# Attention of a block: four heads at a time, or all eight with their matmuls in pairs

## The chip, the core and the metric

The kernel runs on one core of one Trainium2 chip. The metric is the device time of one execution in microseconds; times are medians of several runs. The engines are called as in the profile: PE (matrix engine; PEld its weight loads), DVE (VectorE), ACT (ScalarE), POOL (GpSimd), SP (whose queue starts the transfers).

## What is computed

A decoder layer: RWKV-7 time mixing and sliding-window attention side by side on 2048 positions and 16 meta tokens, then a gated MLP with a convolution. The change is in the attention: eight query heads, two key/value heads (four query heads share one), head size 64, blocks of 128 positions. A query sees the 16 meta keys, the block before and its own (272 columns), a bias by distance, and a sink that takes part in the softmax alone.

```python
s_meta = jnp.einsum('bnqhgd,bmhd->bhgnqm', qb, meta_k)
s_band = jnp.einsum('bnqhgd,bnkhd->bhgnqk', qb, kband)
...
s = jnp.concatenate([s_meta, s_band], axis=-1).astype(jnp.float32) * scale + bias.astype(jnp.float32)
s = jnp.where(mask_all, s, MASK_VALUE)
...
m = jnp.maximum(jnp.max(s, axis=-1, keepdims=True), sink)
e = jnp.exp(s - m)
prob = (e / (jnp.sum(e, axis=-1, keepdims=True) + jnp.exp(sink - m))).astype(v.dtype)
o = (jnp.einsum('bhgnqm,bmhd->bnqhgd', prob[..., :N_META], meta_v)
     + jnp.einsum('bhgnqk,bnkhd->bnqhgd', prob[..., N_META:], vband))
```

## The kernel before

The kernel has two phases. The first does everything up to the residual `h2`, in nine groups of positions: blocks 0 and 1 (block 0 holds the meta tokens, 16 queries), seven groups of two full blocks, and block 16 alone. The second phase is the MLP (tiles up, dn, o).

A group runs the steps of a list, `ORDER` (`FIRST` and `LAST` for the first and last group). A capital letter is the group's own step, a small one the same step of the group before. B and N begin a group (transposes tp, operands xh and xl), F0 to F3 compute the features of a pair of RWKV heads (matmuls g, pz, pa, pg, pss, spr, pb), P0 to P3 prepare the chunk matrices (sc, vp, kbtp), I0 and I1 invert them in 31 steps on DVE (tm, tt) behind transfers (nd, nt, td), C0 and C1 run the recurrence over chunks (xp, ma, cb, yp), K makes queries and keys (g, qt, kt), A is attention, and j or J the output projection (o).

`attention_block` takes a block and a list of halves. A half is the four query heads of one key/value head; its queries and keys lie in partitions 0 to 63 (j = 0) or 64 to 127 (j = 1), the slice `js`. `A00` is the first half of the group's first block, `A01` its second half, `A1` both halves of the second block, one after the other. For each half:

- four score matmuls ps<-kt,q (64 rows, 272 columns), each in a bank of its own, emptied into `pr` by one DVE instruction that adds the bias and takes the maximum (L794);
- a softmax on DVE and ACT (L796 to L806); `pm` holds the probabilities of the meta keys;
- one transpose of `pm` and eight of `pr` (pt), copied out by ACT (L818, L828) and DVE (L826);
- the output `po`: two matmuls with the values of the block before and of its own (po<-pt,vb, 512 columns, 64 output partitions), four with the meta values (po<-pt,metav, 128 columns each), then ah on ACT (L840) and al on DVE (L841).

`pr` has one buffer, so a half's first eviction needs the earlier half's transposes to be through. The tiles ps, pt and po, and those of the P steps (sc, vp, kbtp), share two PSUM banks, the tag "at", handed out in the order of the program text. The score and value matmuls are fp32; each leaves two PE records.

Every matmul goes through a `Queue`: matmuls of one queue keep their order (`qc` has attention, `qp` the P steps, `qb` the chain, `qa` the large products). How the queues are mixed on PE, and all other engines' order, is set when the program is built, by a list scheduler that takes the ready instruction of highest priority; priority follows the program text, and `high_priority` raises it.

## Time and profile before

| | us |
|---|---|
| median of three runs | 3100.51 (3096.43 to 3104.7) |
| the profiled execution | 3101.82 |
| its span | 3100.0 |
| PE busy | 2834.1 (91%) |
| PEld busy | 2396.3 (77%) |
| DVE busy | 2105.8 (68%) |
| ACT busy | 1188.0 (38%) |
| POOL busy | 1107.3 (36%) |

The first phase ends where the first up product starts, at 1611.2 us of the span. A PE record's length overlaps with its neighbours, since matmuls are pipelined; what one costs a full engine is read from its start to the start of the next. A bracket at a row's end tells how long the engine stood idle before it, and what ended that.

### The profile page before, as it was taken

The numbers are of one execution on the slowest core, as the hardware profiler recorded it, in microseconds if no ns is written. First come the engines' busy times: TensorE is split into PE (matmuls) and PEld (weight loads), VectorE is DVE, ScalarE is ACT, GpSimd is POOL, SyncE is SP. The second block draws the span as 40 slices with busy tenths as digits, with TensorE's granted clock in tenths as the row PEclk, the third lists the DMA queues.
The fourth block names the chain that finished last, engine by engine and source line by source line (L and its number), as shares of the span: only waits on it lengthen the run. The fifth ranks groups of instructions, "written<-read, shape, count | busy, mean of one in ns | idle before, by whom it ended". The sixth has DMA issues, their size and how long they took to land.

```text
span 3100.0 us, 55199 instructions
## 1 busy us (share of the span) xinstructions
PE 2834.1 (91%) x19749; PEld 2396.3 (77%) x19749; DVE 2105.8 (68%) x6008; ACT 1188.0 (38%) x2758; POOL 1107.3 (36%) x1246
## 2 busy tenths in 40 slices
PE   6789898989999999999859999999899999989998
PEld 5567586777777776777548898888899999888887
DVE  5576766667666766666758878787655655766666
ACT  3344433334343433333234443434433333433343
POOL 3322311111111111111146665656444444554554
PEclk8799999989999999999969999999999999999999
DMA  6676677557676767776754343434644444565564
GB/s 216 211 213 187 208 233 233 179 166 231 183 242 183 242 186 226 194 228 192 246 209 156 146 153 133 156 129 162 232 149 139 155 156 140 189 215 177 201 212 159
DMA packets 302198, 586.43 MB, mean 189 GB/s; under 512 B 150570, under 2 KB 154266, under 8 KB 301924
## 3 DMA queue, kind: packets, MB, share of 16 engines
q1 hardware_dynamic: 301924, 582.90, 58.0%
q8 instruction: 157, 2.57, 0.3%
q14 instruction: 117, 0.96, 0.1%
HBM read 483.98 MB, written 98.79 MB: 188 GB/s over the span
## 4 chain that ended last, share of the span: by engine, by line
PE 61%; DVE 15%; DMA 13%; issue 3%; ACT 3%; SPq 3%; POOL 1%; DVEq 0%; ACTq 0%; POOLq 0%
PE up L86 17%; PE dn L86 13%; PE g L86 12%; PE o L86 5%; DMA o<-kept 4%; PE po L86 3%; SPq L587 2%; DMA wraw<-in_wup 2%; PE ma L86 2%; DVE t L997 2%; PE ps L86 2%; DVE tw L1058 2%; DMA w<-kept 2%; DVE t L999 1%; DMA nt<-nd 1%
## 5 line engine op out<-in xcount | busy, mean ns | idle before, releaser
L86 PE MATMUL up<-ah,o 128*128 128x386 f32 (+2 forms) x3696 | 882.7, 324 | 49.9 <-DMA o<-kept 29.0
L86 PEld LDWEIGHTS up<-ah,o 128*128 128x128 f32 x3696 | 652.4, 192 | 61.6 <-issue 11.6
L86 PE MATMUL up<-al,o 128*128 128x386 f32 (+2 forms) x1848 | 596.9, 323 | 6.9 <-DVE al L913 6.9
L86 PE MATMUL g<-xh,w 128*128 128x256 f32 x2016 | 425.8, 301 | 18.7 <-ACT w L170 7.3
L86 PEld LDWEIGHTS g<-xh,w 128*128 128x128 f32 x2016 | 334.7, 198 | 51.6 <-issue 19.8
L86 PEld LDWEIGHTS up<-al,o 128*128 128x128 f32 x1848 | 354.8, 192 | 8.8 <-DVE al L913 7.7
L1031 DVE TENSOR_TENSOR acc<-acc,dn 128x512 f32<-128x512 f32 x360 | 242.4, 684 | 114.9 <-PE dn L86 113.9
L86 PE MATMUL dn<-dh,gh 128*128 128x512 f32 x704 | 279.7, 397 | 29.0 <-DVE acc L1031 26.4
L1069 POOL TENSOR_TENSOR o<-wraw,o 128x512 fp32r<-128x512 f32 x198 | 269.5, 1361 | 99.0 <-ACT o L1068 72.2
L86 PE MATMUL g<-xl,w 128*128 128x256 f32 x1008 | 300.2, 298 | 3.1 <-DVE xl L145 3.1
L86 PE MATMUL dn<-dh,gl 128*128 128x512 f32 x704 | 276.6, 393 | 0.7 <-POOL gl L1006 0.7
L86 PE MATMUL dn<-dl,gh 128*128 128x512 f32 x704 | 276.3, 393 | 0.0
L156 POOL TENSOR_TENSOR dl<-wraw,dh 128x1024 fp32r<-128x1024 f32 x66 | 158.7, 2424 | 203.3 <-ACT dh L155 203.3
L997 DVE SCALAR_TENSOR_TENSOR t<-c,cols,t 128x384 f32<-128x384 f32 (+1 forms) x198 | 169.7, 858 | 79.5 <-ACT t L995 77.4
L86 PEld LDWEIGHTS g<-xl,w 128*128 128x128 f32 x1008 | 199.7, 198 | 14.6 <-issue 6.6
L1006 POOL TENSOR_TENSOR gl<-t,gh 128x384 fp32r<-128x384 f32 (+1 forms) x132 | 134.8, 1021 | 145.4 <-ACT gh L1005 145.4
L592 DVE TENSOR_TENSOR tm<-nt,tt 128x60 f32<-128x60 f32 (+36 forms) x558 | 128.9, 231 | 83.2 <-DMA w<-kept 28.3
L86 PEld LDWEIGHTS dn<-dh,gh 128*128 128x128 f32 x704 | 133.1, 189 | 65.4 <-DVE acc L1031 36.0
L676 POOL TENSOR_TENSOR sw<-S,wc 128x128 f32<-128x128 f32 x66 | 28.5, 432 | 421.1 <-DVE S L677 314.8
L1068 ACT ACTIVATE o<-wraw 128x512 fp32r<-128x512 f32 x198 | 121.8, 625 | 132.4 <-PE up L86 117.5
L995 ACT ACTIVATE t<-c,cols 128x384 f32<-128x384 f32 (+1 forms) x198 | 125.9, 667 | 106.9 <-DVE c L1112 102.1
L86 PE MATMUL g<-w,xh 128*128 128x256 f32 (+3 forms) x544 | 151.7, 362 | 13.9 <-ACT w L170 8.3
(283 smaller groups left out, 5672.3 us busy)
## 6 DMA issues: line engine op xcount, KB each, us to landing
w<-kept SPq DMA_DIRECT2D x448, 512.0 KB
o<-kept SPq DMA_DIRECT2D x176, 512.0 KB
wraw<-in_wup SPq DMA_DIRECT2D x88, 512.0 KB
kept<-o SPq DMA_DIRECT2D x88, 512.0 KB
wraw<-in_wdn SPq DMA_DIRECT2D x66, 512.0 KB
kept<-w SPq DMA_DIRECT2D x56, 512.0 KB
wraw<-in_wup SPq DMA_DIRECT2D x44, 256.0 KB
xt<-in_x SPq DMA_DIRECT2D x16, 512.0 KB
```

Source lines behind the costliest of these rows:

```text
L86: self._pin(self.nc.tensor.matmul(*args, **kw))
L156: nc.gpsimd.tensor_tensor(lo, raw, hi.bitcast(F32), op=ALU.subtract)
L587: nc.sync.dma_start(nt[p0:p0 + H], ndv[:, b * 32:b * 32 + 32, b * 32:b * 32 + 32])
L592: V.tensor_tensor(t, bc(nt[0:np_, s, s + 1:32], j, 1), tt[0:np_, 0:j, s:s + 1].to_broadcast([np_, j, m]), op=ALU.mult)
L995: A.activation(o, c[:, 2:half + 2], AF.Identity, bias=cols[:, C_CB + j:C_CB + j + 1], scale=cols[:, C_CW0 + j:C_CW0 + j + 1])
L997: V.scalar_tensor_tensor(o, c[:, 1:half + 1], cols[:, C_CW1 + j:C_CW1 + j + 1], o, op0=ALU.mult, op1=ALU.add)
L999: V.scalar_tensor_tensor(o, c[:, 0:half], cols[:, C_CW2 + j:C_CW2 + j + 1], o, op0=ALU.mult, op1=ALU.add)
L1006: P.tensor_tensor(gl[:, hs], ts[0], gh[:, hs].bitcast(F32), op=ALU.subtract)
L1031: nc.vector.tensor_tensor(t[:, hs], t[:, hs], ps, op=ALU.add)
L1058: V.tensor_tensor(t, x, y, op=ALU.subtract)
L1068: A.activation(hi, w, AF.Copy)
L1069: P.tensor_tensor(lo, w, hi.bitcast(F32), op=ALU.subtract)
```

## The change

`attention_block` takes all eight heads of a block at once, and the list's steps A00 and A01 become one, A0, where A00 stood. `pr`, `m8`, `l8`, `e8`, `pm` are twice as wide, `metav` has 128 partitions, `pt1` and `pt2` have two buffers. Four times, two banks are taken and two score matmuls are issued, one of each half, in partitions 0 to 63 and 64 to 127; the one whose bank was emptied last comes first, and the second has `follow`, a priority raised by 100000. The two halves' value products go to partitions 0 to 63 and 64 to 127 of one bank, in turn. One transpose serves `pm` of all eight heads, one ah and one al the block. The squares of K take `pr`'s buffer, the squares of N take the projection's junk buffer, and in P the two matmuls of a pair change places.

```diff
-ORDER = "B F0 P0 F1 P1 c1 K I0 F2 A00 P2 F3 P3 A01 A1 I1 j C0 N".split()
+ORDER = "B F0 P0 F1 P1 c1 K I0 F2 A0 P2 F3 P3 A1 I1 j C0 N".split()
 LAST = "B F0 P0 F1 P1 c1 F2 P2 I0 F3 K P3 I1 A0 C0 j C1 J".split()
-FIRST = "B F0 P0 F1 P1 I0 K F2 A00 P2 F3 P3 A01 A1 c1 I1 j C0".split()
+FIRST = "B F0 P0 F1 P1 I0 K F2 A0 P2 F3 P3 A1 c1 I1 j C0".split()
...
-    def matmul(self, *args, **kw):
-        self._pin(self.nc.tensor.matmul(*args, **kw))
+    def matmul(self, *args, follow=False, **kw):
+
+        if follow:
+            with self.tc.high_priority(FOLLOW):
+                self._pin(self.nc.tensor.matmul(*args, **kw))
+        else:
+            self._pin(self.nc.tensor.matmul(*args, **kw))
...
-        junk = pool.tile([128, D // 2], mybir.dt.bfloat16, tag="junk", name="junk", bufs=1)
+        junk = pool.tile([128, D // 2], mybir.dt.bfloat16, tag="jk2", name="junk", bufs=1)
...
-        self.metav = ap([64, 4, 128], F32, "metav")
+        self.metav = ap([128, 4, 128], F32, "metav")
...
-                for hd, ps in enumerate(pss):
+                for hd, ps in reversed(list(enumerate(pss))):
...
-            for h in range(1, 4) if b == 0 else ():
-                nc.sync.dma_start(self.metav[16 * h:16 * h + 16, h, :], self.metav[0:16, 0, :])
-            sq = sp.tile([128, 640], F32, tag="qsq", name="qsq")[0:rows]
+            for x in range(1, 8) if b == 0 else ():
+                nc.sync.dma_start(self.metav[16 * x:16 * x + 16, x % 4, :], self.metav[0:16, 0, :])
+            sq = sp.tile([128, 640], F32, tag="pr", name="qsq", bufs=1)[0:rows]
...
-    def attention_block(self, blk, ctx, halves):
+    def attention_block(self, blk, ctx):
...
+        js = [slice(j * 64, j * 64 + 64) for j in range(2)]
...
+        def bank(name):
+            return self.psum.tile([128, 512], F32, tag="at", name=name, bufs=2)
...
-            pr = sp.tile([128, 4, 272], F32, tag="pr", name="pr", bufs=1)
...
-                ps = self.psum.tile([128, 512], F32, tag="at", name="ps", bufs=2)
-                T.matmul(ps[0:nq, 0:nk], self.q[js, h, q0:q0 + nq], kt[js, 0:nk], start=True, stop=True)
...
+        pr = sp.tile([128, 8, 272], F32, tag="pr", name="pr", bufs=1)
+        m8, l8, e8 = [sp.tile([128, 8], F32, tag=t, name=t, bufs=2)[0:nq] for t in ("m8", "l8", "e8")]
+        sink = self.cols[0:nq, C_SINK:C_SINK + 8]
+        for h in range(4):
+            pss = [bank("ps") for _ in range(2)]
+            turn = ((1, 0), (0, 1))[h % 2]
+            for j in turn:
+                T.matmul(pss[j][0:nq, 0:nk], self.q[js[j], h, q0:q0 + nq], kt[js[j], 0:nk], start=True, stop=True,
+                         follow=j == turn[1])
+            for j in turn:
+                ps, x = pss[j], 4 * j + h
...
-                    V.tensor_tensor_reduce(pr[0:nq, h, 0:nk], ps[0:nq, 0:nk], bt, 1.0, sink[:, h:h + 1],
-                                           ALU.add, ALU.max, m4[:, h:h + 1])
...
+                    V.tensor_tensor_reduce(pr[0:nq, x, 0:nk], ps[0:nq, 0:nk], bt, 1.0, sink[:, x:x + 1],
+                                           ALU.add, ALU.max, m8[:, x:x + 1])
+        V.tensor_tensor(e8, sink, m8, op=ALU.subtract)
+        V.tensor_scalar(m8, m8, -1.0, None, op0=ALU.mult)
+        A.activation(e8, e8, AF.Exp)
...
+        pm = sp.tile([128, 8, 16], F32, tag="pm", name="pm")[0:nq]
+        V.tensor_tensor(pm, pr[0:nq, :, 0:16], bc(l8, 16, 2), op=ALU.mult)
+        for x in range(8) if b else ():
+            V.tensor_scalar(pr[:, x, 16:], pr[:, x, 16:], l8[:, x:x + 1], None, op0=ALU.mult)
...
+            po0, pv = pt0, ps[:, 0:128]
+            T.transpose(pv, pm.rearrange("p h k -> p (h k)"), self.ident)
...
-                for c, (pt, vv) in enumerate(zip(pts, (vprev, vb))):
-                    T.matmul(ps[js], vv[:, js], pt, start=c == 0, stop=False)
-                for h in range(4):
-                    T.matmul(po[:, h, :], self.metav[:, h, js], pt0, start=False, stop=h == 3)
-            hv = ctx["ah"][js, :, q0:q0 + nq]
-            A.activation(hv, po, AF.Copy)
-            V.tensor_tensor(ctx["al"][js, :, q0:q0 + nq], po, hv.bitcast(F32), op=ALU.subtract)
...
+                pts[c].append(pt)
+        ps = bank("po")
+        po = ps.rearrange("p (h t) -> p h t", h=4)[:, :, 0:nq]
...
+            for c, vv in enumerate((vprev, vb)):
+                for j in range(2):
+                    T.matmul(ps[js[j]], vv[:, js[j]], pts[c][j], start=c == 0, stop=False, follow=j == 1)
+            for h in range(4):
+                for j in range(2):
+                    T.matmul(po[js[j], h, :], self.metav[js[j], h, js[j]], pt0[js[j]], start=False, stop=h == 3,
+                             follow=True)
+        hv = ctx["ah"][:, :, q0:q0 + nq]
+        A.activation(hv, po, AF.Copy)
+        V.tensor_tensor(ctx["al"][:, :, q0:q0 + nq], po, hv.bitcast(F32), op=ALU.subtract)
```

What the scheduler makes of it is seen on PE. Behind P3 of a group with two full blocks come, before, the scores of the first block's second half. They stand alone among g's and chain steps (ps are scores; ma and cb the chain; the number is that of the tile):

```order
L86 MATMUL ps_8154<-kt2_117,q_7387 128x272
L86 MATMUL g_8879<-xl_8784,w_8880 128x256
L86 MATMUL g_8879<-xh_8783,w_8880 128x256
L86 MATMUL g_8879<-xh_8783,w_8894 128x256
L86 MATMUL ps_8157<-kt2_117,q_7387 128x272
L86 MATMUL ma_8644<-vu_6755,kbt_6950 64x64 x2
L86 MATMUL ma_8644<-vu_6755,kbt_7156 64x64 x2
L86 MATMUL cb_8645<-vu_6755,ms_6926 64x64 x2
L86 MATMUL cb_8645<-vu_6755,ms_7132 64x64 x2
L86 MATMUL g_8879<-xl_8784,w_8894 128x256
```

There, after, come the scores of the second block:

```order
L92 MATMUL ps_8089<-kt3_118,q_7284 128x272
L92 MATMUL ma_8470<-vu_6652,kbt_6847 64x64 x2
L92 MATMUL ma_8470<-vu_6652,kbt_7053 64x64 x2
L92 MATMUL cb_8471<-vu_6652,ms_6823 64x64 x2
L92 MATMUL cb_8471<-vu_6652,ms_7029 64x64 x2
L90 MATMUL ps_8088<-kt3_118,q_7284 128x272
L92 MATMUL ps_8094<-kt3_118,q_7284 128x272
L92 MATMUL ma_8505<-S0_127,ar_6811 64x64 x2
L92 MATMUL ma_8505<-S0_127,ar_7017 64x64 x2
L92 MATMUL ma_8505<-vu_6652,ms_6823 64x64 x2
L92 MATMUL ma_8505<-vu_6652,ms_7029 64x64 x2
L92 MATMUL cb_8506<-S0_127,ar_6811 64x64 x2
```

Tiles ps_8089 and ps_8088 are a pair (heads of j = 1 and j = 0), 8094 and 8095 the next, 8101 the first of the third. The four steps of ma and of cb have come between the two of a pair, and no g is left between the scores.

At the first block's first scores, behind the key transposes of the same group, before:

```order
L86 MATMUL g_7764<-xl_6586,w_7779 128x256
L86 MATMUL g_7764<-xh_6585,w_7779 128x256
L89 MATMUL kt_7574<-ident_61,qk_7456 128x128
L86 MATMUL ps_7847<-kt2_117,q_7387 128x272
L86 MATMUL ps_7850<-kt2_117,q_7387 128x272
L86 MATMUL g_7960<-xh_6585,w_7961 128x256
```

And after:

```order
L95 MATMUL qt_7465<-ident_61,qk_7353 128x128 x4
L92 MATMUL ps_7745<-kt2_117,q_7284 128x272
L90 MATMUL ps_7744<-kt2_117,q_7284 128x272
L95 MATMUL kt_7471<-ident_61,qk_7353 128x128
L92 MATMUL g_7931<-xh_6482,w_7932 128x256
L92 MATMUL g_7931<-xl_6483,w_7932 128x256
```

The two of before read the same rows, heads 0 and 1 of j = 0; the two of after are a pair of both halves and stand before kt.

The output of a half on PE in a group with two full blocks, before:

```order
L86 MATMUL g_9045<-xh_8783,w_9046 128x256
L86 MATMUL ma_8714<-S0_127,ar_6914 64x64
L86 MATMUL po_8196<-pt2_8194,vb2_121 64x512
L86 MATMUL po_8196<-pt0_8178,metav_123 64x128 x4
L86 MATMUL ps_8209<-kt3_118,q_7387 128x272
L86 MATMUL ma_8714<-S0_127,ar_6914 64x64
```

And the output of the second block of the group that stands above, after:

```order
L92 MATMUL po_8167<-pt1_8144,vb2_121 64x512
L90 MATMUL po_8167<-pt1_8151,vb2_121 64x512
L92 MATMUL po_8167<-pt2_8158,vb3_122 64x512
L92 MATMUL g_8775<-xh_8644,w_8790 128x256 x2
L92 MATMUL g_8775<-xl_8645,w_8790 128x256
L92 MATMUL g_8775<-xh_8644,w_8790 128x256 x2
L92 MATMUL g_8775<-xl_8645,w_8790 128x256
L92 MATMUL g_8775<-xh_8644,w_8790 128x256
L92 MATMUL pz_8819<-wa_8769,dup_106 128x256
L92 MATMUL pa_8823<-wa_8769,dup_106 128x256
L90 MATMUL po_8167<-pt2_8165,vb3_122 64x512
L90 MATMUL po_8167<-pt0_8135,metav_123 64x128 x8
```

Before, the second value product and the four meta products of the half stand together, and the next half's scores behind them. After, three value products stand together, the fourth comes behind g, pz and pa, and then the eight meta products. From the first up product on, PE's order is the same in both programs.

## Rows read from the trace of the kernel before

**Rows 1.** Busy time by stretch: us, PE PEld DVE ACT POOL, PEclk, DMA share, GB/s.
```profile
300.00:1500.00 1200.00, 1130.02 (x9810) 872.23 (x9810) 820.97 (x3406) 462.86 (x1349) 192.03 (x288) 0.96 0.69 210
1500.00:1611.00 111.00, 71.41 (x490) 48.63 (x488) 68.80 (x236) 32.50 (x89) 26.05 (x23) 0.71 0.64 221
1611.00:3100.00 1489.00, 1400.38 (x7736) 1292.63 (x7736) 1030.57 (x1622) 573.69 (x993) 802.05 (x815) 0.98 0.48 166
```

**Rows 2.** PE groups, whole span: xcount | busy us, mean ns | idle before, releasers.
```profile
L86 PE MATMUL ps<-kt,q 64*128 64x272 f32 (+1 forms) x272 | 93.3, 435 | 6.1 <-DVE m L794 5.6 <-ACT vu L562 0.2 <-DVE tm L592 0.2
...
L86 PE MATMUL po<-pt,vb 128*64 128x512 f32 x128 | 67.2, 627 | 1.6 <-DVE last L419 1.5
```

**Rows 3.** PE in time order, 711 to 717: start us, us, what, xcount [idle before <-releaser].
```profile
712.90 0.72 PE L86 MATMUL ps<-kt,q 64*128 64x272 f32 x2
713.55 0.39 PE L86 MATMUL g<-xl,w 128*128 128x256 f32 x1
713.78 0.40 PE L86 MATMUL g<-xh,w 128*128 128x256 f32 x2
714.01 0.28 PE L86 MATMUL g<-xl,w 128*128 128x256 f32 x1
...
716.31 0.45 PE L86 MATMUL ma<-vu,kbt 128*64 128x64 f32 x8
716.59 0.40 PE L86 MATMUL cb<-vu,ms 128*64 128x64 f32 x8
```

**Rows 4.** PE in time order, 730 to 737.
```profile
731.13 1.07 PE L86 MATMUL po<-pt,vb 128*64 128x512 f32 x2
732.13 0.70 PE L86 MATMUL pg<-gd,gup 128*128 128x256 f32 x2
...
736.03 1.08 PE L86 MATMUL po<-pt,metav 64*64 64x128 f32 x8
737.04 0.72 PE L86 MATMUL ps<-kt,q 64*128 64x272 f32 x2
```

**Rows 5.** PE in time order, 754 to 756.
```profile
754.38 1.90 PE L86 MATMUL po<-pt,vb 128*64 128x512 f32 x4 [1.53 <-DVE last L419]
756.21 1.08 PE L86 MATMUL po<-pt,metav 64*64 64x128 f32 x8
```

**Rows 6.** PE in time order, 678 to 680.
```profile
678.79 0.70 PE L86 MATMUL pz<-wa,dup 64*128 64x256 f32 x2
679.42 0.93 PE L86 MATMUL xp<-T,ms 32*32 32x32 f32 x30
```

**Rows 7.** PE in time order, 725 to 726.
```profile
725.06 0.48 PE L86 MATMUL pz<-wa,dup 64*128 64x256 f32 x1
725.07 0.48 PE L86 MATMUL pa<-wa,dup 64*128 64x256 f32 x1
...
725.69 0.39 PE L86 MATMUL g<-xh,w 128*128 128x256 f32 x1
```

**Rows 8.** PE in time order, 1511 to 1512.
```profile
1511.12 0.45 PE L86 MATMUL ma<-S,ar 64*64 64x64 f32 x8
1511.40 0.40 PE L86 MATMUL ma<-vu,ms 64*64 64x64 f32 x8
```

**Rows 9.** Waits of PE from 300 to 1500: us in total, times, longest us.
```profile
PE ps L86 <- DVE m L794: 4.3, 1, 4.3
```

**Rows 10.** DVE groups of phase 1: xcount | busy us, mean ns | idle before, releasers.
```profile
L794 DVE CUSTOM_DVE_ANT_0 pr<-ps,bias,cols 128x272 f32<-128x272 f32 x120 | 59.3, 497 | 41.1 <-PE ps L86 40.4
...
L841 DVE TENSOR_TENSOR al<-po,ah 64x512 fp32r<-64x512 f32 (+1 forms) x34 | 22.4, 659 | 13.7 <-ACT ah L840 13.2
```

**Rows 11.** PE in time order, 1530 to 1537, the last group's second half.
```profile
1530.03 0.72 PE L86 MATMUL ps<-kt,q 64*128 64x272 f32 x2 [0.60 <-DVE m L794]
...
1535.01 0.66 PE L89 MATMUL yp<-ident,yt 128*128 128x128 f32 x2 [2.82 <-ACT pr L800]
1536.75 0.42 PE L89 MATMUL pt<-ident,pm 128*64 128x128 f32 x1 [1.08 <-DVE pm L804]
```

More of the change, by code (lines that the diff above doesn't have):

```diff
@@ L41 @@
 WBUF, QKB = 5, 2
+FOLLOW = 100000
 GN = 256
@@ L248, in bank @@
             return self.psum.tile([128, 512], F32, tag="at", name="psb", bufs=2)
-        anti = sp.tile([128, 4, 272], F32, tag="pr", name="anti", bufs=1)[:, 0, 0:128]
+        anti = sp.tile([128, 8, 272], F32, tag="pr", name="anti", bufs=1)[:, 0, 0:128]
         nc.sync.dma_start(anti, a["cst"][:, 128:256])
@@ L380, in step @@
             if i < len(ctx["blocks"]):
-                self.attention_block(ctx["blocks"][i], ctx, [int(x) for x in step[2:]] or [0, 1])
+                self.attention_block(ctx["blocks"][i], ctx)
         else:
@@ new lines, in attention_block @@
+        V.tensor_tensor(e8, sink, m8, op=ALU.subtract)
+        V.tensor_scalar(m8, m8, -1.0, None, op0=ALU.mult)
+        A.activation(e8, e8, AF.Exp)
+        for x in range(8):
+            A.activation(pr[0:nq, x, 0:nk], pr[0:nq, x, 0:nk], AF.Exp, bias=m8[:, x:x + 1], accum_out=l8[:, x:x + 1])
+        V.tensor_tensor(l8, l8, e8, op=ALU.add)
+        V.reciprocal(l8, l8)
+        pm = sp.tile([128, 8, 16], F32, tag="pm", name="pm")[0:nq]
+        V.tensor_tensor(pm, pr[0:nq, :, 0:16], bc(l8, 16, 2), op=ALU.mult)
@@ new lines, in attention_block @@
+        for x in range(8) if b else ():
+            V.tensor_scalar(pr[:, x, 16:], pr[:, x, 16:], l8[:, x:x + 1], None, op0=ALU.mult)
+        pt0 = sp.tile([128, 128], F32, tag="pt0", name="pt0")
+        ps = bank("pt")
+        if b == 0:
+            po0 = pt0[0:16].rearrange("p (h t) -> p h t", h=8)
+            pv = ps[0:16, 0:128].rearrange("p (h t) -> p h t", h=8)
+            for x in range(8):
+                T.transpose(pv[:, x, :], pm[:, x, :], self.ident[0:nq, 0:nq])
+        else:
+            po0, pv = pt0, ps[:, 0:128]
+            T.transpose(pv, pm.rearrange("p h k -> p (h k)"), self.ident)
@@ L825, in attention_block @@
+        A.activation(po0, pv, AF.Copy)
+        pts = []
+        for c in range(2 if b else 0):
+            pts.append([])
+            for j in range(2):
+                ps = bank("pt")
+                for h in range(4):
+                    T.transpose(ps[:, h * 128:h * 128 + 128], pr[:, 4 * j + h, 16 + c * 128:144 + c * 128], self.ident)
+                pt = sp.tile([128, 512], F32, tag="pt%d" % (c + 1), name="pt%d" % (c + 1), bufs=2)
                 if c == 0:
@@ L828, in attention_block @@
                     A.activation(pt, ps, AF.Copy)
[L829 to L841 removed]
+                pts[c].append(pt)
+        ps = bank("po")
+        po = ps.rearrange("p (h t) -> p h t", h=4)[:, :, 0:nq]
+        if b == 0:
+            for j in range(2):
+                T.matmul(po[js[j]], self.metav[0:16, 0, js[j]], po0[:, 4 * j:4 * j + 4, :], start=True, stop=True)
+        else:
+            for c, vv in enumerate((vprev, vb)):
+                for j in range(2):
+                    T.matmul(ps[js[j]], vv[:, js[j]], pts[c][j], start=c == 0, stop=False, follow=j == 1)
+            for h in range(4):
+                for j in range(2):
+                    T.matmul(po[js[j], h, :], self.metav[js[j], h, js[j]], pt0[js[j]], start=False, stop=h == 3,
[3 more added lines that the diff above has]
+        V.tensor_tensor(ctx["al"][:, :, q0:q0 + nq], po, hv.bitcast(F32), op=ALU.subtract)
     def project(self, ctx):
```

56 lines of the change are left out of this document (7 added, 49 removed).

## The prediction

> **What bounds the kernel now.** I read first the busy time by stretch [rows 1]. In the middle of the first phase, 300 to 1500 us, where most of the sixteen full attention blocks lie, the matmul engine is busy 1130 of 1200 us (94%), with 70 us idle. VectorE is busy 821 of these 1200 us (68%), ScalarE 463, and the DMA engines 0.69. The granted clock is 0.96 on average. So in this stretch a microsecond taken from the matmul engine's stream is a microsecond of time, as long as no new wait comes up for it. From 1500 to 1611 us, the last group, it is busy only 71 of 111 us at a granted clock of 0.71: there waits decide. The second phase, from 1611 us, is not touched: from the first up product on, the order of the matmul engine's instructions is the same in both programs. Next I read the groups of the engine's work [rows 2]. The scores (ps<-kt,q) keep it busy 93.3 us and the products with the values (po<-pt,vb) 67.2 us. Last, the engine in order of time [rows 3 to 8] gives the slots, from one start to the next, which is what an instruction costs a full engine. The records come in two for each of these matmuls (x2 is one matmul).
>
> **The prices.** A score matmul that stands alone between g's takes 0.65 us (712.90 to 713.55), and the g behind it 0.23 us (713.55 to 713.78), where two g's in a row take 0.23 (713.78 to 714.01): so each break of the g stream costs another 0.11 us [rows 3]. A value product alone takes 1.00 us (731.13 to 732.13) [rows 4], two of them 1.83 us (754.38 to 756.21) [rows 5]. The four products with the meta values of one half take 1.01 us (736.03 to 737.04) [rows 4].
>
> **Does a pair run side by side?** The trace of before already has each kind of pair, elsewhere. Different rows: pz alone takes 0.63 us (678.79 to 679.42) [rows 6]; pz and pa, which read rows 0 to 63 and 64 to 127 and write two banks, take together 0.63 us (725.06 to 725.69), started 10 ns apart [rows 7]. The second one is free. Different columns: four ma<-vu,kbt of 64 columns, the column half alternating, take 0.28 us (716.31 to 716.59) [rows 3]; one behind the other at the value products' price, 64/512 of 1.83/2, they would take 0.46. Rows and columns both, into one bank: four ma<-S,ar take 0.28 us (1511.12 to 1511.40) [rows 8], against 0.51 at the meta products' price (1.01 for four of twice the columns). So I count a pair at the price of one.
>
> On this last kind a rule of the Trainium skill speaks against the change: TensorEngine Tiling (Array Packing), section Gotcha 1: PSUM Pressure, has it that matmuls in different row tiles cannot use the same PSUM bank at the same time. The pairs of meta products do that, in the bank po. The trace disagrees, since the ma<-S,ar pairs of [rows 8] share the bank ma and still take about half. By the rule the 16 us of the meta products below would be missing, and the sum would be 3066.
>
> **What is really paired.** The order of the changed program says how far the edit gets. Of the 64 pairs of full score matmuls only 25 stand directly one behind the other; in the other 39 the scheduler has put one to twenty-one matmuls between, in spite of the priority. Of the 16 blocks' four value products, five blocks have all four in a row, eleven have three and one. The eight meta products of a block are always in a row.
>
> **The sum on the matmul engine.**
> - Scores: 25 second ones free, 25 x 0.65 = 16.3 us. Off this, before had 20 score matmuls directly behind another and after has about 8 outside pairs, at 0.11 to 0.2 us of spared entry each (the price of a break, or twice it): 2 us. Takes away 14.
> - Value products: before 34 alone and 15 twos, 34 x 1.00 + 15 x 1.83 = 61.5 us. After, three in a row are a pair and one that waits for its columns, 1.83; so 11 x (1.83 + 1.00) + 5 x 1.83 = 40.3. Takes away 21.
> - Meta products: 32 halves x 1.01 become 16 blocks x 1.01. Takes away 16.
> - Breaks: the stretches of g and o matmuls fall in number from 489 to 401, 88 x 0.11. Takes away 10.
> - The transposes of pm fall from 32 to 16; each lies between nothing and the 0.28 us record of a g [rows 3]. Takes away 2.
>
> Together 63 us. VectorE loses 16 of the al subtractions (0.66 us each, 11 us) [rows 10], and it and ScalarE lose a half's small softmax steps in each block; neither is full, so this counts nothing itself, but it is cover for the waits below. The scheme of the banks, the shared buffer for squares and pr, the shared junk buffer (ScalarE alone writes it) and the four more small DMAs of the meta values in the first group are put at nothing: K's squares are read long before the first scores exist, and the DMAs lie among weight loads in a stretch that fills the engine only in part.
>
> **The last group.** There the second half of the block begins only when the first is through, and the matmul engine stands 2.82 and 1.08 us for it [rows 11]. With one pass for eight heads this goes: 4 us off, at most (what is late next is chain C0 beside it).
>
> **What it adds: waits for banks.** A pair takes both "at" banks, so the next pair waits until VectorE has emptied both, 2 x 0.497 us and what is queued between [rows 10]. Behind the waiting matmul stand all the engine's matmuls, the chain's (ma, cb) too. In the first block of a group some 15 g's lie between pairs, and the wait is covered. In the second block (seven groups) and in the last group's block chain steps alone lie between, 8 to 12 short ones. Before has this case in the last group: scores with nothing between wait 0.60 us [rows 11]. In the g stream its price is near nothing: 4.3 us in one wait in 1200 us [rows 9]. The ends are 0 and 16 blocks x 3 x 1.0 = 48 us. I take 8 blocks x 3 x 0.7 = 17 us, near the dense row, because the order there is dense.
>
> So 63 + 4 - 17 = 50 us less. The profiled execution took 3101.82 us with a span of 3100.0, the median of three is 3100.51; 50 off the median is 3050 us.
>
> **Rivals.**
> - Banks decide everywhere: every pair, also in the g stream, waits for its two evictions, 64 x 1.0 = 64 us. For it: VectorE is busy 68% and carries the inversion's steps between the evictions. Against it: 4.3 us of such waits now [rows 9]. Time: 3100 - 67 + 64 = 3097. The skill has this as a rule: TensorEngine Tiling (Array Packing), section PSUM Bottleneck, says that tiling speeds up the matmuls and not the emptying of PSUM; by it the 0.65 us pair would hide behind 1.0 us of eviction. The trace agrees only in the dense stretch of [rows 11].
> - The change doesn't do what it says: neighbours wait on semaphores of their own and run one after the other. Then only spared entries (25 x 0.15 = 4), 2 of the value products, breaks 10, pm 2 and the last group's 4 remain, 22 us, less 17: 3095. For it: 39 of 64 pairs are not even neighbours. Against it: pz and pa have a wait each and overlap [rows 7].
> - Slower: block A0 now stands whole ahead of P2 in the "at" banks' program order; before, only its first half did. A half takes 24 us from its first score (712.90) to the next half's (737.04) [rows 3, 4]. If the engine has too little other work between A0 and P2, P2, the inversions and the next chain are late by up to that in each of seven groups: 3100 - 67 + 7 x 24 = 3201. It decides once g and o matmuls ready there are fewer than 24 us. Against it: project's o matmuls stand there in the order, and A01's half is gone from behind P3, so the banks' loop gets shorter as a whole.
> - More than forecast: the shorter loop also takes part of the 70 idle us of [rows 1], some 40: 3010.
>
> **How the numbers follow.** Forecast 0.70, with 3020 to 3085 (waits 0 to 48 us); banks 0.10; no overlap 0.06; slower 0.07; more 0.07. A measurement of this kernel can tell about 0.3% from no change, 9 us: faster is below 3091, slower above 3110. Faster 0.70 + 0.07 + 0.03 of the second and third case = 0.80; same 0.12; slower the 0.07 and 0.01 of the banks' case. The range of 8 in 10 leaves out the slow case and the lower half of the last: 3015 to 3097.
>
> **What would show it.** In the profile after: neighbouring ps records that start some 10 ns apart and take 0.65 us together; eight meta products in about 1.0 us; po<-pt,vb busy near 45 us and ps near 78; the matmul engine's busy share of 300 to 1500 still over 0.90, with the first phase ending near 1560 instead of 1611. Idle before ps charged to VectorE's evictions well over 17 us would speak for the banks; a late sc of P2 with idle before it, for the slow case; pairs whose starts lie 0.2 us or more apart, for no overlap. A first phase over 1605 us would make the prediction wrong.

## The result, and the profile after

The changed kernel takes 3146.3 us where the kernel before, measured beside it, takes 3102.6 us: a ratio of 1.0141, 95% interval 1.0108 to 1.0174. It is slower by 44 us. The forecast was 3050 us, its range 3015 to 3097, and only a chance of 0.08 was given to slower.

First the stretches, as in [rows 1]; columns: stretch, its length in us, then busy us of PE, PEld, DVE, ACT, POOL (records in brackets), the granted clock, DMA share, GB/s.

```profile
300.00:1500.00 1200.00, 1096.01 (x9533) 859.77 (x9534) 771.02 (x3180) 453.63 (x1297) 185.91 (x276) 0.91 0.66 200
1500.00:1649.90 149.90, 102.16 (x746) 72.32 (x744) 95.47 (x362) 42.24 (x118) 30.43 (x36) 0.80 0.69 242
1649.90:3147.80 1497.90, 1405.17 (x7736) 1295.44 (x7736) 1028.83 (x1625) 574.73 (x992) 805.45 (x816) 0.98 0.47 166
```

The first phase ends at 1650 us instead of 1611. The second phase, whose order did not change, is 9 us longer in this execution (1498 against 1489); over the profiled executions of all kernels below it lies between 1489 and 1506, so differences of that size between single executions say nothing of an edit. In the 1200 us from 300 on the matmul engine starts 9533 matmul records; before it started 9810 [rows 1]. Its idle time there rises from 70 to 104 us, and the granted clock falls from 0.96 to 0.91. The clock has two levels, 1.2 and 2.4 GHz, so a mean of 0.91 is 1200 x 0.09 / 0.5 = 216 us at the lower one, where before had 96.

The pairs themselves are there. The engine in order of time, in the first block of a group (start, us, what, xcount). Each of these matmuls leaves two records, so x2 is one matmul, and in a pair the records of the two alternate:

```profile
642.16 0.49 PE L92 MATMUL ps<-kt,q 64*128 64x272 f32 x1
642.17 0.49 PE L90 MATMUL ps<-kt,q 64*128 64x272 f32 x1
642.49 0.39 PE L92 MATMUL ps<-kt,q 64*128 64x272 f32 x1
642.50 0.39 PE L90 MATMUL ps<-kt,q 64*128 64x272 f32 x1
642.82 0.33 PE L95 MATMUL kt<-ident,qk 128*128 128x128 f32 x1
...
677.43 0.64 PE L92 MATMUL po<-pt,vb 128*64 128x512 f32 x1
677.43 0.64 PE L90 MATMUL po<-pt,vb 128*64 128x512 f32 x1
...
678.34 1.02 PE L92 MATMUL po<-pt,vb 128*64 128x512 f32 x2
...
680.79 1.09 PE L90 MATMUL po<-pt,metav 64*64 64x128 f32 x16
681.72 0.38 PE L92 MATMUL sc<-ar,kb 64*64 64x128 f32 x2
```

Two scores take 0.66 us (642.16 to 642.82), started 10 ns apart; two value products 0.91 us (677.43 to 678.34); eight meta products 0.93 us (680.79 to 681.72), where before four took 1.01 [rows 4].

To see where the time went, I added up the first phase of each profiled run from the starts in its trace: a slot is start to next start, less the idle time that the next one shows. All columns but the last are us of the whole first phase; the granted clock is that of 300 to 1500 us. The kernels e1 to e18 are those of the experiments below.

| kernel | scores | value | meta | all other slots | idle | phase ends | granted clock |
|---|---|---|---|---|---|---|---|
| before | 85.7 | 63.3 | 31.3 | 1253 | 162 | 1611 | 0.96 |
| changed | 79.8 | 42.4 | 15.4 | 1292 | 205 | 1650 | 0.91 |
| e11 (shared scratch alone) | 86.2 | 64.5 | 32.8 | 1263 | 200 | 1661 | 0.93 |
| e1 (move alone) | 85.7 | 65.7 | 32.6 | 1260 | 173 | 1633 | 0.95 |
| e5 (pairs alone) | 81.0 | 35.9 | 18.6 | 1270 | 172 | 1593 | 0.95 |
| e18 (pairs and move) | 76.6 | 37.1 | 18.7 | 1261 | 174 | 1583 | 0.95 |

The attention's matmuls gave back 43 us, close to the 51 forecast for them. All other matmuls, which are the same ones but for 16 transposes fewer, cost 39 us more, and idle time 43 us more.

The 39 us can be set against the clock. Added up by the granted clock under which they ran, the other slots stood at the lower level for 159 us before and for 256 us in the changed kernel. Two g's in a row take 0.42 us there (893.71 to 894.13 in the changed kernel) and 0.23 us at the upper level [rows 3]. So 97 us more at the lower level are, as an estimate from these two prices, 97 x (1 - 0.23 / 0.42) = 44 us of longer slots. That covers the 39.

Where the idle time is. Waits of the matmul engine from 300 to 1500 us (us in total, times, longest), first of before beside [rows 9], then of the changed kernel:

```profile
PE ma L86 <- DVE S L677: 8.1, 5, 3.1
...
PE g L86 <- DMA w<-kept: 3.5, 3, 2.7
```

```profile
PE ma L92 <- DVE S L683: 15.9, 4, 4.4
PE g L92 <- DMA w<-kept: 11.8, 5, 4.5
PE ps L92 <- DVE m L806: 8.8, 3, 6.0
...
PE g L92 <- DVE vb L747: 5.8, 2, 4.2
PE ps L90 <- DVE m L806: 4.8, 6, 1.2
...
PE ps L92 <- ACT vu L568: 3.4, 5, 1.2
```

No one of them carries the loss. The longest single wait among them, first on the matmul engine, then on VectorE, in the second block of a group:

```profile
879.27 0.39 PE L92 MATMUL ps<-kt,q 64*128 64x272 f32 x1
879.27 0.39 PE L90 MATMUL ps<-kt,q 64*128 64x272 f32 x1
879.62 0.45 PE L92 MATMUL ma<-S,ar 64*64 64x64 f32 x8
879.90 0.40 PE L92 MATMUL ma<-vu,ms 64*64 64x64 f32 x8
880.14 0.40 PE L92 MATMUL cb<-S,ar 64*64 64x64 f32 x8
886.49 1.27 PE L92 MATMUL ps<-kt,q 64*128 64x272 f32 x2 [5.96 <-DVE m L806]
887.70 1.11 PE L95 MATMUL tp<-ident,xt 128*128 128x128 f32 x4
888.74 1.27 PE L90 MATMUL ps<-kt,q 64*128 64x272 f32 x2
```

```profile
878.62 0.75 DVE L128 TENSOR_SCALAR xt<-xt,rs 128x1024 f32<-128x1024 f32 x1
879.28 0.28 DVE L683 TENSOR_TENSOR S<-ma,sw 128x128 f32<-128x128 f32 x1
885.12 0.19 DVE L598 TENSOR_TENSOR tm<-nt,tt 128x31 f32<-128x31 f32 x1 [5.55 <-DMA nt<-nd]
...
885.94 0.49 DVE L806 CUSTOM_DVE_ANT_0 pr<-ps,bias,cols 128x272 f32<-128x272 f32 x1
```

A pair of scores at 879.27 fills both banks. VectorE, which must empty them, stands in order behind a step of the inversion that waits 5.55 us for a DMA (nt<-nd). So the next score, and every matmul behind it, waits 5.96 us. When the engine goes on, a score takes 1.27 us instead of 0.72 [rows 3] and its four transposes 1.11: it is at the lower level, and the stretch from 877 to 897 us has a granted clock of 0.74. So this stall is paid twice: as 5.96 us of idle time, and in the slots of the 9 us of work behind it, by the prices of two g's some 4 us more (an estimate).

### The profile page after: what moved, and what is told of

The parts are those of the page before. It is cut to its first block, busy times and chain, and to the rows that moved or that the text cites. A ratio compares the mean times of both kernels' runs of the same rounds, so it can differ in the third digit from the quotient of the medians.

```text
span 3147.8 us, 54960 instructions
## 1 busy us (share of the span) xinstructions
PE 2835.0 (90%) x19733; PEld 2410.9 (77%) x19733; DVE 2079.9 (66%) x5906; ACT 1181.9 (38%) x2707; POOL 1107.2 (35%) x1246
## 4 chain that ended last, share of the span: by engine, by line
PE 58%; DVE 16%; DMA 14%; issue 4%; ACT 3%; SPq 3%; POOL 2%; DVEq 0%; ACTq 0%; POOLq 0%
PE up L92 16%; PE g L92 13%; PE dn L92 12%; PE o L92 5%; DMA o<-kept 3%; DMA w<-kept 3%; PE ma L92 2%; DMA wraw<-in_wup 2%; DVE tw L1076 2%; DVE t L1015 2%; SPq L593 2%; DVE t L1017 1%; DVE tm L598 1%; PE pt L95 1%; PE sc L92 1%
## 5 line engine op out<-in xcount | busy, mean ns | idle before, releaser
L92 PEld LDWEIGHTS up<-ah,o 128*128 128x128 f32 x3696 | 651.6, 191 | 65.7 <-ACT cu L1113 10.2
L92 PE MATMUL g<-xh,w 128*128 128x256 f32 x2016 | 435.8, 308 | 34.3 <-DMA w<-kept 11.8
L92 PEld LDWEIGHTS g<-xh,w 128*128 128x128 f32 x2016 | 347.4, 206 | 62.5 <-issue 18.8
L92 PE MATMUL g<-xl,w 128*128 128x256 f32 x1008 | 308.1, 306 | 4.4 <-DVE xl L151 4.4
L92 PEld LDWEIGHTS g<-xl,w 128*128 128x128 f32 x1008 | 208.3, 207 | 20.4 <-issue 8.7
L92 PEld LDWEIGHTS dn<-dh,gh 128*128 128x128 f32 x704 | 134.5, 191 | 66.1 <-DVE acc L1049 36.4
```

What stands on the lines that cost most here:

```text
L92: self._pin(self.nc.tensor.matmul(*args, **kw))
```

## The experiments

All ratios are to the kernel before, run beside each, with their 95% intervals. Theories: PLACE (the first block's attention now stands whole ahead of the seventh strip), PAIRS (the pairing makes the loss), BUFFERS or SCRATCH (the shared buffers do), SCHEDULE (each edit makes the scheduler draw another order of all engines' work, and the order of before is a good one), WIDE (softmax of eight heads as one step takes the pairs' gain), CLOCK (what the pairs save comes back as lower clock and waits). The expectations call step P2 of `ORDER` the seventh strip, P3 the eighth, and P0 of the next group its first. Where a ratio is said to be over or under 1, its interval leaves 1 out.

**Move alone, on the kernel before.**

```
-ORDER = "B F0 P0 F1 P1 c1 K I0 F2 A00 P2 F3 P3 A01 A1 I1 j C0 N".split()
+ORDER = "B F0 P0 F1 P1 c1 K I0 F2 A0 P2 F3 P3 A1 I1 j C0 N".split()
```

> The kernel before with one edit: the whole attention of a group's first block stands ahead of the seventh projection strip (A0 for A00 there, and A01 left out behind P3); the halves are still taken one after the other and no matmul is paired. Theory PLACE (the loss lies in where the step now stands: the second half's eight softmax and value steps go ahead of the seventh strip, and the stretch behind the eighth strip then holds only the second block): slower than before by at least the 44 us that the changed kernel lost, 3146 to 3190, since here no shorter attention pays any of it back, with over 200 us of low granted clock in the first phase. Theory PAIRS (the pairing itself, its held bank pairs and its priority, makes the loss): within 10 us of before, 3093 to 3113, and the low clock stays near its 235 us.

1.0127 (1.0086 to 1.0169). Slower, but by less than the changed kernel plus its gain, and its clock stays at 0.95: PLACE in the sharp form I gave it does not fit, and PAIRS fits no better.

**Parts of the pairing undone in the changed kernel.** e2 takes the priority out:

```
-        if follow:
+        if False:
```

e3 takes the four scores of one half, then of the other, one bank each:

```
-        for h in range(4):
-            pss = [bank("ps") for _ in range(2)]
...
+        for j in range(2):
+            for h in range(4):
+                x, ps = 4 * j + h, bank("ps")
+                T.matmul(ps[0:nq, 0:nk], self.q[js[j], h, q0:q0 + nq], kt[js[j], 0:nk], start=True, stop=True)
```

e4 moves the second block behind the next group's first strip (a1; in FIRST and LAST likewise):

```
-ORDER = "B F0 P0 F1 P1 c1 K I0 F2 A0 P2 F3 P3 A1 I1 j C0 N".split()
+ORDER = "B F0 P0 a1 F1 P1 c1 K I0 F2 A0 P2 F3 P3 I1 j C0 N".split()
```

> The changed kernel with its priority for the second matmul of a pair taken away; all else stays, so pairs may be torn apart by other work. Theory PAIRS, in the form that the priority pulls work forward and lets it wait for banks in front of ready work: 3100 to 3115, most of the loss comes back. Theory PLACE: the loss stays, and the value and meta products lose some of their overlap: 3146 to 3175 (up to 30 us of the 37 us that the value and meta products gained).

> The changed kernel with its score matmuls unpaired: the four of the first half and then the four of the second, each with one bank of its own, as before; value and meta products stay paired, the step stays where it is. Theory PAIRS, in the form that two banks taken at once by each pair of scores leave the softmax no bank to drain while the next is filled: 3105 to 3125, and the idle time of score matmuls behind the evictions falls from about 14 us to the 5 us of before. Theory PLACE: 3140 to 3155, since the scores gained only about 6 us by pairing and the rest is untouched.

> The changed kernel with the attention of a group's second block moved from behind the eighth projection strip to behind the first strip of the next group, where the gate and output products of the next strips stand beside it; the pairing stays. Theory PLACE (the stretch behind the eighth strip has nothing to fill the waits of the second block's softmax chain): the first phase loses most of its 110 us of idle time there, and the kernel falls to 3060 to 3110. Theory PAIRS: the loss goes with the pairs wherever they stand, 3130 to 3160.

1.0109 (1.0057 to 1.0162), 1.0116 (1.0071 to 1.0162) and 1.0239 (1.0195 to 1.0282). Neither priority nor held bank pairs carry the loss: both variants stay over 1%. The second block is not helped by other surroundings; e4 is the slowest of all.

**Pairs alone, in the old place.** To pair without moving, a half-step takes two heads of each half instead of four of one.

```
-        for j in halves:
+        for g in halves:
+            hs = slice(2 * g, 2 * g + 2)
...
-                    T.matmul(ps[js], vv[:, js], pt, start=c == 0, stop=False)
+                    for j in range(2):
+                        T.matmul(ps[js[j], 0:256], vv[:, js[j]], pt[:, 256 * j:256 * j + 256], start=c == 0,
+                                 stop=False, follow=j == 1)
```

> The kernel before with the pairing alone: its steps stand where they stood (A00 ahead of the seventh strip, A01 behind the eighth), its buffers keep their sizes, but a half-step now takes two heads of each half instead of four heads of one half, so that its score matmuls stand in pairs on different rows and its value and meta products in pairs on different columns. The value products have 256 columns instead of 512 and are twice as many, so the work is the same. Theory PLACE (moving the step makes the loss, the pairs gain by themselves): faster than before by 20 to 45 us, 3055 to 3080, since the value and meta products save up to 37 us of slots and nothing is moved. Theory PAIRS: slower than before by 10 us or more. Third, CLOCK (what the pairs save comes back as lower granted clock and waits, wherever they stand): within 12 us of before, with the slot sum of the first phase 20 us or more lower and its low clock time 40 us or more higher.

0.9969 (0.9949 to 0.9989). Faster, by 10 us: under the 20 to 45 of PLACE, and against PAIRS. Its slots are 28 us lower in sum, its idle time 10 higher. That is near CLOCK, but the time at the lower level in the first phase rose by 24 us (235 to 259), not by 40. The meta products of this kernel pair on other columns alone, and the transposes of `pm` stay at 32.

**The changed kernel with its first block elsewhere**: both blocks behind the eighth strip (e6, first line that is added), or the first between the seventh and eighth (e7, second).

```
-ORDER = "B F0 P0 F1 P1 c1 K I0 F2 A0 P2 F3 P3 A1 I1 j C0 N".split()
+ORDER = "B F0 P0 F1 P1 c1 K I0 F2 P2 F3 P3 A0 A1 I1 j C0 N".split()
+ORDER = "B F0 P0 F1 P1 c1 K I0 F2 P2 F3 A0 P3 A1 I1 j C0 N".split()
```

> The changed kernel with the attention of both blocks of a group behind the eighth strip (order F2 P2 F3 P3 A0 A1), so that nothing of it stands ahead of the seventh strip. Theory PLACE, in the form of the slower case of the prediction (the whole first block's attention ahead of the seventh strip puts off that strip's inversion and with it the chain): the delay is gone, 3090 to 3120. Against it, in the form that the stretch behind the eighth strip runs out of filling work: it now holds twice as much attention and less beside it, 3150 to 3200.

> The changed kernel with the first block's attention between the seventh and the eighth strip (order F2 P2 F3 A0 P3 A1). If the seventh strip's delay behind the attention makes the loss: 3100 to 3130. If it is the eighth strip that must not come late, or the spacing of the steps as such: 3140 to 3170.

1.0105 (1.0074 to 1.0136) and 1.0101 (1.0073 to 1.0130). The loss stays over 1% at either place: a late seventh strip is not it.

**The small edits alone, on the kernel before**: all three (e8), then each: the squares in the softmax buffer (e9), two score matmuls of the inversion in reverse (e10), one scratch for two norms (e11).

```
-            sq = sp.tile([128, 640], F32, tag="qsq", name="qsq")[0:rows]
+            sq = sp.tile([128, 1088], F32, tag="pr", name="qsq", bufs=1)[0:rows, 0:640]
...
-                for hd, ps in enumerate(pss):
+                for hd, ps in reversed(list(enumerate(pss))):
...
-        junk = pool.tile([128, D // 2], mybir.dt.bfloat16, tag="junk", name="junk", bufs=1)
+        junk = pool.tile([128, D // 2], mybir.dt.bfloat16, tag="jk2", name="junk", bufs=1)
```

> The kernel before with the changed kernel's small edits alone: the square of the projected heads takes the buffer of the softmax rows instead of its own, one scratch tile shares another's buffer, and the inversion's two halves are started in reverse order; attention stays unpaired and in its place. Theories PLACE and PAIRS: within 8 us of before. Rival BUFFERS (the shared buffers make the attention's features wait for the softmax of the block before): slower by 15 us or more.

> The kernel before with one of the three small edits alone: the square of the projected heads (qsq) takes the buffer of the softmax rows (pr). The instructions of every engine stand in the same order as before, so only the new waits for that buffer differ. Theory BUFFERS (that shared buffer makes the loss of the small edits): slower by 20 to 36 us, 3121 to 3137, with the wait of gate products for DVE's vb eviction at about 15 us as in the run with all three edits. Theory SCHEDULE (any edit gives the scheduler another order, and the order of before is a better one than most): within 8 us of before, since here the order is the same.

> The kernel before with another of the small edits alone: of the two inversion score matmuls of each piece, the second half's is issued first. The same matmuls, banks and buffers; but the order of the engines' work comes out of the scheduler with thousands of lines moved. Theory BUFFERS: within 8 us of before, 3093 to 3109. Theory SCHEDULE: slower by 15 to 40 us, 3116 to 3141, with no one wait that carries it and 30 us or more of further low clock in the first phase.

> The kernel before with the last of the small edits alone: the scratch output of the row norms shares a buffer with the scratch output of the last norms, which nothing reads. Theory BUFFERS: within 8 us of before. Theory SCHEDULE: slower by 15 to 40 us, as any other order would be.

All three: 1.0116 (1.0079 to 1.0152). Squares: 1.0002 (0.9984 to 1.0020), with the order of every engine as before. Reverse: 1.0077 (1.0053 to 1.0100). Scratch: 1.0141 (1.0114 to 1.0169), as much as the whole change. So BUFFERS falls for the squares, beside a softmax of four heads. The scratch has a mechanism in the trace. VectorE's scaling of the normed blocks and the transposes that read it, first of before, then of e11 (count, ns min/median/max, first and last start):

```profile
L89 PE MATMUL tp<-ident,xt x136: 272/273/475, 15.9 to 1378.2; 128*128 128x128 f32 x128, 64*128 64x64 f32 x8
L122 DVE TENSOR_SCALAR xt<-xt,rs x17: 742/747/755, 15.1 to 1235.1; 128x1024 f32<-128x1024 f32 x16, 64x1024 f32<-64x1024 f32 x1
```

```profile
L89 PE MATMUL tp<-ident,xt x136: 272/417/477, 14.9 to 1425.1; 128*128 128x128 f32 x128, 64*128 64x64 f32 x8
L122 DVE TENSOR_SCALAR xt<-xt,rs x17: 737/747/1741, 14.1 to 1422.7; 128x1024 f32<-128x1024 f32 x16, 64x1024 f32<-64x1024 f32 x1
```

and ScalarE's and the matmul engine's waits up to 1600 us, before and e11 again (us in total, times, longest):

```profile
ACT jk L870 <- DVE xr L866: 42.3, 14, 13.4
ACT junk L118 <- DMA xt<-in_x: 20.0, 7, 5.9
PE tp L89 <- DVE xt L122: 15.9, 1, 15.9
```

```profile
ACT jk L870 <- DVE xr L866: 68.3, 16, 13.5
ACT junk L118 <- DMA xt<-in_x: 2.5, 1, 2.5
PE tp L89 <- DVE xt L122: 35.1, 5, 14.9
PE g L86 <- DVE vb L741: 21.0, 4, 6.3
```

Before, the norms run ahead: the last block is scaled at 1235 us, and ScalarE waits there for the next x to arrive. With one scratch the norm of a group (junk) comes only behind the last norms (jk) of the output products; the last block is scaled at 1423 us, 2.4 us before its last transposes. Matmuls now wait for it (35.1 us against 15.9), and half of the transposes take over 0.41 us instead of 0.27. The changed kernel has the same sign:

```profile
L128 DVE TENSOR_SCALAR xt<-xt,rs x17: 744/749/1773, 14.3 to 1416.8; 128x1024 f32<-128x1024 f32 x16, 64x1024 f32<-64x1024 f32 x1
```

**The one edit undone, and further orders.** e12 is the changed kernel with the two score matmuls of the inversion in the order of before; e13 and e14 are e5 with the edits of e10 and e11; e15 is e1 with that of e10; e16 is e5 without priority. The diffs are those above.

> The changed kernel with one small edit undone: the two inversion score matmuls of each piece in the order of before. If that edit carries loss of its own: 3110 to 3130. If it is one of many orders of about the same worth (SCHEDULE) or the loss is the buffer's or the place's: 3130 to 3160.

> The kernel with the pairs in place (e5) and the empty edit of e10 on top (the order of two inversion score matmuls). If the pairs are worth about the 1% that their slots showed, and the rest is the order that an edit draws (before alone having a good one): 3.09 to 3.12 ms, that is 25 to 45 us under the same two edits on the kernel before (3124 and 3146). If e5 was itself a lucky order and pairs are worth nothing: 3120 to 3150. If order is not it and e10 costs 0.8% by itself: 3110 to 3120.

> The kernel with the pairs in place (e5) and the empty edit of e11 on top (a scratch output shares a buffer). Pairs worth about 1%, the rest order: 3090 to 3125. Pairs worth nothing, e5 lucky: 3120 to 3150. If the shared scratch costs by itself what it cost on the kernel before (48 us): 3135 to 3145.

> The kernel with the move alone (e1) and the empty edit of e10 on top. If the move has a price of its own (theory PLACE) beside that of another order: 3140 to 3175, the sum of both. If the move costs only what any other order costs (theory SCHEDULE): 3115 to 3145, no further loss on top of e1's 3133.

> The kernel with the pairs in place (e5) without the priority for the second of a pair. If the priority is what makes the pairs overlap: value and meta slots of the first phase go back from 55 us towards the 95 us of before, 3100 to 3130. If most pairs stand together anyway: slots within 8 us of e5's, and the time only that of another order, 3090 to 3125.

e12 1.0112 (1.0088 to 1.0136); e13 0.9928 (0.9908 to 0.9948); e14 1.0088 (1.0069 to 1.0106); e15 1.0101 (1.0071 to 1.0131); e16 0.9981 (0.9963 to 0.9999). The reverse edit costs 0.8% on the kernel before, gains 0.4% with the pairs, and in the changed kernel and with the move its 0.3% either way is within the noise: it has no price of its own, and about half a per cent either way is what another order is worth. The scratch costs 1.2% on the pairs (1.0088 / 0.9969), near its 1.4% on before. With the reversal and the squares there already it costs only 0.4% (e8 against e10), so its price is not the same in every kernel, and these edits change the order too. Without priority the value and meta slots stay at 55 us (36.4 and 19.0): the pairs stand together anyway.

**The scratch undone in the changed kernel.**

```
-        junk = pool.tile([128, D // 2], mybir.dt.bfloat16, tag="jk2", name="junk", bufs=1)
+        junk = pool.tile([128, D // 2], mybir.dt.bfloat16, tag="junk", name="junk", bufs=1)
...
-                    junk = sp.tile([128, 512], mybir.dt.bfloat16, tag="jk2", name="jk2", bufs=1)
+                    junk = sp.tile([128, 512], mybir.dt.bfloat16, tag="pt1", name="jk2", bufs=2)
```

> The changed kernel with one small edit undone: the row norms have their own scratch buffer again, as before; to make room, the scratch of the last norms lies in one of the buffers of the transposed softmax rows, which are idle then. Theory SCRATCH: the 1.2 to 1.4% that the edit cost in two other kernels comes back, 3095 to 3115, and the wait of PE's transposes for the normed block (tp behind DVE xt) falls from 19 us to the 15 us of before. Theory SCHEDULE: one more order like the others, 3130 to 3150. In between, 3115 to 3130, the edit and the move each carry a part.

1.0155 (1.0127 to 1.0184). A miss for SCRATCH as the whole cause. Undone, its sign is gone (the last block is scaled at 1250.7 us again, the wait for it is 14.6 us), and the time has not come back: other waits are there in its place. Waits of its matmul engine up to 1600 us, then one of ScalarE:

```profile
PE g L92 <- DVE vb L747: 26.4, 6, 4.7
PE g L92 <- DMA w<-kept: 18.8, 18, 2.5
PE cb L92 <- ACT yt L688: 16.4, 7, 3.4
...
PE tp L95 <- DVE xt L128: 14.6, 1, 14.6
...
PE g L92 <- DVE xr L884: 10.4, 7, 3.7
```

```profile
ACT jk L888 <- PE po L90: 7.2, 6, 2.1
```

The last of each may come from the buffer that this run lends to the scratch: ScalarE now waits there for the value products to be through. So this run does not clear the edit in the changed kernel, and it does not show that the edit costs anything there. Squares with a buffer of their own beside the softmax rows of eight heads weren't tried.

**Pairs in half-steps, at the changed kernel's place**: e5 with the ORDER of e1.

> The kernel with the pairs in place (e5), with its two half-steps one behind the other ahead of the seventh strip, where the changed kernel has its whole block. Theory WIDE (one softmax of eight heads, with its bursts of eight evictions and eight exponentials, takes the pairs' gain; the place costs what e1 and e15 show): 3098 to 3118, 0.0 to 0.5% over before, the 1.1% of the place less the 0.8% of the pairs. Theory PLACE (at that place shorter matmuls buy nothing, whatever the width): 3130 to 3150, as the changed kernel.

0.9903 (0.9873 to 0.9933), 3076.0 us: the fastest of all, faster than both kernels. PLACE falls. The figure of WIDE (3098 to 3118) was missed too, on the fast side: with the pairs the move cost nothing. Its stretches:

```profile
300.00:1500.00 1200.00, 1120.96 (x10151) 881.96 (x10150) 817.83 (x3473) 470.88 (x1382) 192.89 (x293) 0.95 0.72 217
1500.00:1583.00 83.00, 42.85 (x268) 30.36 (x267) 46.17 (x143) 22.38 (x57) 20.41 (x17) 0.66 0.52 186
```

At the same place, with the same pairs but for the meta products (other columns alone), the engine starts 10151 records in the 1200 us instead of 9533, at a granted clock of 0.95. Its waits of scores for VectorE are 5.0 us there, where the changed kernel has 13.6:

```profile
PE ps L89 <- DVE m L807: 4.0, 3, 2.4
...
PE ps L91 <- DVE m L807: 1.0, 1, 1.0
```

**The parts, each at equal other edits** (differences of the ratios, in %):

| edit | on | worth |
|---|---|---|
| pairs in half-steps | before, + reverse, + scratch, + move | -0.3, -1.5, -0.5, -2.2 |
| move | before, + reverse, + pairs | +1.3, +0.2, -0.7 |
| scratch | before, + pairs, + reverse and squares, in the changed kernel (e17, with its lent buffer) | +1.4, +1.2, +0.4, -0.1 |
| reverse | before, + pairs, + move, in the changed kernel (e12) | +0.8, -0.4, -0.3, +0.3 |

A difference of two such ratios is uncertain by 0.3 to 0.5. Pairs gain each time, 1.1% (35 us) in the mean. The move and the reverse have no sign of their own. The scratch loses clearly in two kernels, and not in the other two. All eight kernels with the softmax of eight heads as one step stand at 1.010 or more, e17 with its own scratch too; of the five with pairs in half-steps the four with their own scratch are under 1.

From the half-steps (0.9903) to the changed kernel (1.0141) it is 2.4%. What is left between the two is the step of eight heads, the shared scratch, the squares' buffer, the reversal and the order that came of them all. How the 2.4% divide is not shown: the scratch's part may be anything from nothing (e17) to some 1.3% (e11, e14), the reversal's 0.3% is within the noise, and the step of eight heads was never measured without the other edits.

## Why the prediction was wrong

- **The price of a pair: right.** 0.66, 0.91 for two value products and 0.93 for eight meta products were forecast as 0.65, 1.00 and 1.01. The value products gave 21 us (forecast 21), the meta products 16 (16). The scores gave 6 of 14: they stood at the lower level for 23 us instead of 9, which by the prices of a score there and at the upper level (1.21 us, 886.49 to 887.70, against 0.65) is some 6 of the missing 8 (an estimate). The rule of the Trainium skill that was weighed, TensorEngine Tiling (Array Packing), Gotcha 1: PSUM Pressure, is not what this trace shows: the meta products, of two row halves and two column halves, overlap in one bank (0.93 us for eight, where four took 1.01).
- **My test by busy time was badly chosen.** Scores near 78 and value products near 45 us were to show it. The rows have 52.7 + 51.9 and 34.8 + 32.4, since two records that run side by side count twice; only the slots show the gain. The other sign, a busy share over 0.90 from 300 to 1500 us, came true (1096 of 1200) in a kernel that is slower, while the first phase ended at 1650 us, past the 1605 that was to make the prediction wrong:

```profile
L90 PE MATMUL ps<-kt,q 64*128 64x272 f32 (+1 forms) x136 | 52.7, 470 | 5.7 <-DVE m L806 4.8 <-ACT kbt L575 0.9
L92 PE MATMUL ps<-kt,q 64*128 64x272 f32 (+1 forms) x136 | 51.9, 465 | 12.6 <-DVE m L806 9.1 <-ACT vu L568 3.4
...
L90 PE MATMUL po<-pt,vb 128*64 128x512 f32 x64 | 34.8, 640 | 0.0
L92 PE MATMUL po<-pt,vb 128*64 128x512 f32 x64 | 32.4, 631 | 0.0
```

- **Waits for banks: the size was near, the reason half right.** 17 us were forecast on top of before. By the rows above scores wait 17 us (8.8 + 4.8 + 3.4) in the stretch where they waited 4.5 (4.3 of them in [rows 9]), so 12.5 were added. All but one wait of 1.75 us stand where I put them, in the second block. Eight of the nine waits for VectorE are 0.4 to 1.75 us, like the 0.7 of the forecast. The longest, 5.96 us, is for a VectorE that stands behind a DMA, and not for the evictions' own length.
- **The step that failed: slots taken as time.** The first paragraph says that a microsecond taken from the stream is a microsecond of time as long as no new wait comes up, and then prices one wait, at 17 us. The 43 us gained in the attention's slots were lost twice: 43 us of new idle time, of which the scores' waits are 12.5 and the rest is spread over many others, and 39 us in all other slots. A term for the lower clock was missing altogether, and by the estimate above it is worth the whole 39.
- **Under it: edits put at nothing.** "The shared junk buffer (ScalarE alone writes it)" was put at nothing, with no reason but that one engine writes it. One buffer ties the order of its writers: the norm of the next group no longer runs ahead of the last norms. By itself that edit cost 1.4% and 1.2% in two kernels, 44 and 37 us. In the changed kernel its sign is there, but undoing it (e17) brought nothing back, so its share of the 44 us is not shown. Nor is that of the step of eight heads, whose fewer small steps the prediction counted as cover for the waits. Which of them starts the new waits stays open.
- **The last group** was to give 4 us and gave none. The two waits of 2.82 and 1.08 us [rows 11] have become one, for the softmax of eight heads:

```profile
1570.01 0.48 PE L95 MATMUL pt<-ident,pm 128*128 128x128 f32 x1 [4.50 <-DVE pm L816]
```

- **The breaks** (10 us) can't be seen under the longer slots.
- **The rivals.** The slower one named the moved step as its mechanism. The time came out slower, but the place is not why: with pairs in half-steps the same place is the fastest, and the changed kernel loses over 1% with its first block at two other places (e6, e7). "No overlap" is wrong by the rows above, and so is "banks decide everywhere": 17 us of such waits are not 64. The rule of the Trainium skill behind that rival (TensorEngine Tiling (Array Packing), PSUM Bottleneck) holds in the second block almost alone, as where the pair at 879.27 waits to be emptied.
- **The forecast itself.** Pairs gave 10 to 69 us at equal other edits, 35 in the mean. That e18 came to 3076, inside the range, does not bear the 50 us out: it is another kernel, and an order that it drew is in the number too. The slots of the pairs were sized about right; what the rest of the edit does to waits and clock was left out.

## What to carry to other kernels

Price every line of a diff, the ones that only make room too: a buffer shared by two steps of one engine can tie a step that ran ahead to one that waits. Before an edit's gain is believed or its loss explained, measure an edit that changes only the order; here that alone moved the time by up to 0.8%, as much as most gains. And when a wider step gains in its matmuls, try it at the old width: pairs across the halves did not need all eight heads at once.

## What the runs showed of the hardware

Three kinds of pairs overlap: scores on other rows (two in 0.66 us), value products on other columns (two in 0.91 us), and meta products on other rows and other columns in one bank (eight in 0.93 us). After a stall of some 6 us the matmul engine came back at its lower level (a score 1.27 us instead of 0.72), for about 9 us in that place. In the changed kernel the slots of the untouched matmuls grew by 39 us beside 43 us of new idle time; 97 us more of them stood at the lower level, which is worth 44 us by the estimate above. Two rows of a profile whose matmuls run side by side each count the same time (52.7 + 51.9 us for the scores, 93.3 before), so busy time does not show such a gain.
